# A fp32 decoder trunk on one core: eight pairs of weight tiles only in the FFNs, and four of eight k pairs in seven products in two of eleven groups

## The chip, the cores and the metric

The kernel runs on one core of one Trainium2 chip. The metric is the device time of one execution in microseconds (us); the time of a kernel is the median of its runs. A second number, the span, comes from one profiled execution and runs from its first to its last profiled instruction.

## What is computed

A decoder trunk over 256 positions of width 2048, all in float32: two layers, then a last RMSNorm.

```python
def swiglu(xn, w_gate, w_up, w_down):
    return (jax.nn.silu(xn @ w_gate) * (xn @ w_up)) @ w_down
...
for layer in range(DEPTH):                       # DEPTH = 2
    xn = rms_norm(h, norm_mix[layer])
    if layer % 2 == 0:
        mix = swa_mlstm_mixer(xn, w_in_even[j], w_out_even[j], ...)
    else:
        mix = forgetting_attention_mixer(xn, w_in_odd[j], fox_b_f[j], w_out_odd[j])
    h = h + mix
    h = h + swiglu(rms_norm(h, norm_ffn[layer]), w_gate[layer], w_up[layer], w_down[layer])
return rms_norm(h, norm_final)
```

The first mixer (the even layer) is sliding-window attention beside an mLSTM, the second (the odd layer) softmax attention with forget gates. Each ends in an output projection, `@ w_out`, 2048 to 2048. The FFN goes from 2048 to 5632 and back.

## The kernel before, in words

**Precision.** Every fp32 operand stands as two fp32r tiles, hi and lo. A weight chunk (256 rows by 512 columns, 512 KB) is loaded by SP into a raw tile (line 132; pool `wr`, four buffers). `split_chunk` (line 182) makes the pair: ACT copies raw to hi (line 185), DVE subtracts hi from raw to lo (line 186). A product of blocks is then three matmuls: hi·hi, hi·lo, lo·hi (lines 220 to 222 in `gemm`, lines 530 to 532 in `three`).

**Weight tiles.** `slot` (line 106) hands out the pairs of the list `weights` in turn. Six pairs are made once for the whole kernel, in pool `wp` (line 104). `close_layer` (line 762) opens the pool `fp0` or `fp1` of a layer's end, makes two more pairs there (hi6, lo6, hi7, lo7) and appends them to the list; then it runs `out_proj`, then `ffn`, then takes them off again. The pool of the layer's end opens while the mixer still works, in memory that it gives up; a tile whose memory is still read waits for the last reader.

**Output projection.** `out_proj` (line 508) works in 512-column blocks of w_out, two at a time: for both blocks the first 12 of the 16 k steps, then for both the last 4. A block is 8 chunks of 12 matmuls. Its left operand is mh and ml, the mixer's result, of which the early k steps (the attention heads) are there sooner than the late ones. Finished blocks are added to the residual (line 368), and xh and xl for the FFN are made of them by two batches of four transposing DMAs a block pair (`box`, line 315, on SP). The mixer's end in the even layer is the mLSTM (lines 1079 to 1130), whose output goes through transposing DMAs (`hv`, line 333) to mh (line 359); in the odd layer it is the softmax (lines 418 to 431), the transposes of its probabilities (lines 471 and 475) and the products with v (lines 485 and 486).

**FFN.** `ffn` (line 635) takes w_gate and w_up in 11 groups of 512 columns, in three parts (0 to 2, 3 to 6, 7 to 10); after each part come the down products of what is done. A group is a call of `pair_group` (line 537) over eight pairs of k steps. A plain pair is 24 matmuls. In a mixed pair the 2 x 2 blocks of the pair are multiplied in seven products in place of eight, 21 matmuls: DVE forms sums of the weight blocks (lines 605 to 608), of which one extra half tile and two full tiles are split (line 355) beside the usual split of one chunk. A mixed pair takes four pairs of weight tiles, a plain one two. The sums on the activation side (`sx`, `x4`) are made once a layer. At a group's end, `combine` (line 551) joins the seven-product banks and line 663 adds the plain banks. Plain and product banks are four PSUM banks each, which change roles from group to group (`bank`, line 534).

`ORDER` says which pairs are mixed and in what order they come; `HEAVY` has four mixed pairs, and a mixed pair first. `DENSE` names the groups that use HEAVY; it is empty, so that all use ORDER:

```python
ORDER = ((0, 0), (1, 1), (0, 2), (1, 3), (0, 4), (1, 5), (0, 6), (0, 7))
HEAVY = ((1, 1), (0, 0), (1, 3), (0, 2), (1, 5), (0, 4), (1, 7), (0, 6))
```

**Order of the work.** Each engine runs its instructions in program order, and that order is fixed when the program is built: the framework's scheduler interleaves them by when it takes tiles and operands to be free. So a change of which tile a chunk gets can reorder every engine.

Of the kernel before, what the change touches and what calls it, by code (L numbers as in the profile page):

```python
# [9 lines left out]
F32R = mybir.dt.float32r  # L10
# [7 lines left out]
P = 128  # L18
# [5 lines left out]
NB = 512  # L24
CK = 2
# [10 lines left out]
ORDER = ((0, 0), (1, 1), (0, 2), (1, 3), (0, 4), (1, 5), (0, 6), (0, 7))  # L36
HEAVY = ((1, 1), (0, 0), (1, 3), (0, 2), (1, 5), (0, 4), (1, 7), (0, 6))
FOURTH = 7
DENSE = ()
DOWN = {  # L40
    6: ((0, 0), (1, 1), (0, 2), (1, 3), (0, 4), (0, 5)),
    8: ((0, 0), (1, 1), (0, 2), (1, 3), (0, 4), (1, 5), (0, 6), (0, 7)),
# [26 lines left out]
def mixed_of(order):  # L69
    return [p for w, p in order if w]  # L70
# [5 lines left out]
def trunk(  # L76
# [23 lines left out]
    xl = sp_.tile([P, KT, S], F32R, name="xl")  # L100
    mh = sp_.tile([P, KT, S], F32R, name="mh")
    ml = sp_.tile([P, KT, S], F32R, name="ml")
    wp = ctx.enter_context(tc.tile_pool(name="wp", bufs=1))
    weights = [[wp.tile([P, CK, NB], F32R, name=f"{a}{i}") for a in ("hi", "lo")] for i in range(6)]

    def slot():
        weights.append(weights.pop(0))
        return weights[-1]

    wr = ctx.enter_context(tc.tile_pool(name="wr", bufs=4))  # L110
    cp = ctx.enter_context(tc.tile_pool(name="cp", bufs=1))
# [70 lines left out]
    def split_chunk(raw, n):  # L182
        hi, lo = slot()
        for k in (slice(0, 1), slice(1, CK)) if any(raw is f for f in fine) else (slice(0, CK),):
            latest[0] = nc.scalar.copy(hi[:, k, 0:n], raw[:, k, 0:n])  # L185
            nc.vector.tensor_tensor(  # L186
                out=lo[:, k, 0:n], in0=raw[:, k, 0:n], in1=hi[:, k, 0:n].bitcast(F32), op=ALU.subtract
            )
        return hi, lo
# [318 lines left out]
    def out_proj(w, idx, key, extra):  # L508
        last, rest = KT - 4, []
        for n0 in (0, 2):  # L510
            accs = [new_acc() for _ in range(2)]
            for i in range(2):
                gemm(accs[i], m_of, w, (n0 + i) * NB, NB, 0, last, KT, step=6 * i)
            for i in range(2):
                gemm(accs[i], m_of, w, (n0 + i) * NB, NB, last, KT, KT, step=6)
                add_out(accs[i], n0 + i)
                (later if n0 == 0 else rest).append(
                    (LATER[n0 + i], split_turned(idx, n0 + i, *scrap(extra[3], n0 + i), extra))
                )
                square_sum(key, n0 + i)  # L520
        return rest
# [15 lines left out]
    def pair_group(fp, par, lhs, sums, mats, order, todo=(), halves=None, inner=None, raws=None):  # L537
# [32 lines left out]
        for pos, (kind, pair) in enumerate(order):  # L570
# [21 lines left out]
            if first:  # L592
# [8 lines left out]
                else (t4[:, 0, :], t4[:, 1, :], ra[:, 0, :], ra[:, 1, :])  # L601
            )
            hu, lu = slot()
            split_plain(hu[:, 1, :], lu[:, 1, :], rb[:, 1, :])
            nc.vector.tensor_tensor(out=ta, in0=rb[:, 0, :], in1=ra[:, 0, :], op=ALU.subtract)
# [4 lines left out]
            for src in (ra, rb) if halves else (t4, ra):  # L610
                if halves:
                    hs, ls = halves.pop(0)
                    halves.append((hs, ls))
                else:
                    hs, ls = slot()
                split_plain(hs, ls, src)
                parts.append((hs, ls))
# [17 lines left out]
    def ffn(layer, fp, sx, x4, sd, key, todo, idx_next=None, key_next=None, finish=None):  # L635
# [8 lines left out]
        for g0, g1 in zip(PARTS, PARTS[1:]):  # L644
# [3 lines left out]
            for g in range(g0, g1):  # L648
# [6 lines left out]
                    [(w_gate[layer], g * NB), (w_up[layer], g * NB)],  # L655
                    HEAVY if g in DENSE else ORDER,
                    todo,
# [104 lines left out]
    def close_layer(layer, w_out, idx, key, **rest):  # L762
        with tc.tile_pool(name=f"fp{layer}", bufs=2) as fp:
            nx = len(mixed_of(ORDER))
            nd = max(len(mixed_of(o)) for o in DOWN.values())
            sx = [fp.tile([P, nx, 4, P], F32R, name=f"sx{i}", bufs=1) for i in range(2)]
            x4 = fp.tile([P, 2, P], F32R, name="x4", bufs=1)
            more = [[fp.tile([P, CK, NB], F32R, name=f"{a}{i}", bufs=1) for a in ("hi", "lo")] for i in (6, 7)]
            weights.extend(more)
            todo = out_proj(w_out, idx, key, (*sx, x4, fp))  # L770
            sd = [fp.tile([P, nd, 4, P], F32R, tag=f"sd{i}", name=f"sd{i}", bufs=1) for i in range(2)]
            ffn(layer, fp, sx, x4, sd, key, todo, **rest)
            for pair in more:
                weights.remove(pair)


    acc0 = new_acc()
    hi, lo = slot()
# [366 lines left out]
    for n in range(4):  # L1145
        nc.gpsimd.dma_start(h[:, :, n * NB : (n + 1) * NB], xv[:, :, n * NB : (n + 1) * NB])

    close_layer(0, w_out_even[0], 2, "f0", idx_next=1, key_next="m1")


# [140 lines left out]
    def finish(acc, n, gf):  # L1291
        for t in range(NT):
# [31 lines left out]
            nc.scalar.dma_start(ov[:, t, NB : 2 * NB], b1)  # L1324

    close_layer(1, w_out_odd[0], 3, "f1", finish=finish)


# [47 lines left out]
```

## Time and profile before

| | before |
|---|---|
| median of 3 runs | 2105.7 us (2105.07 to 2107.09) |
| the profiled execution | 2104.5 us, span 2102.8 us |
| mean granted TensorE clock | 0.993 |
| HBM read | 408.68 MB, 195 GB/s over the span |

How to read it: PE is TensorE's matmuls, PEld its weight loads (beside PE), DVE VectorE, ACT ScalarE, SP the engine that issues the DMAs; SPq marks an issue on it. A row of the timeline is start, duration, engine, line, operation, output tile <- input tiles; in brackets the idle time before it and what ended it. A row of a group of instructions is line, engine, operation, count | busy time, mean in ns | idle before, and what ended it. A row of waits is engine, tile and line that waited <- what it waited for: us in all, times, longest. A row of windows is the stretch and its length, then busy time (instructions) of PE, PEld, DVE, ACT and POOL, the granted clock, the share of the DMAs and GB/s. Of the 40 slices of the span, PE is at nine tenths or more in all but the fifth, the 26th and the last, and the granted clock in all but the 26th.

### The profile page before, as it was taken

What the parts mean: (1) busy time and instruction counts of PE and PEld (TensorE: products, weight loads), DVE (VectorE), ACT (ScalarE), POOL (GpSimd) and SP (SyncE); (2) the same over time, 40 slices, a digit from 0 to 9 for tenths busy, and PEclk for the clock granted to TensorE, in tenths of its full rate; (3) what the DMA queues carried; (4) which work ended last, traced back from release to release, by engine and by line L of the source; (5) the groups of instructions that cost most, each with busy time, mean ns of one, the idle gap of its engine ahead of it and who ended that gap; (6) DMA issues with size and microseconds to landing.
All of it is one profiled execution on the core that took longest, in us unless ns stands there. A gap on an engine that the chain in (4) does not pass through costs nothing.

```text
span 2102.8 us, 26924 instructions
## 1 busy us (share of the span) xinstructions
PE 2072.5 (99%) x9473; PEld 1718.5 (82%) x9473; DVE 1821.5 (87%) x2367; ACT 1373.8 (65%) x1744; POOL 41.4 (2%) x66
## 2 busy tenths in 40 slices
PE   9999899999999999999999999899999999999998
PEld 7878688888888888888888888688888888888887
DVE  6788668999999899999898778579999999899994
ACT  6767577665576656667676776577655667556763
POOL 1010100000000000000000000000000000000000
PEclk9999999999999999999999999899999999999999
DMA  8566577666677567766677866476756677666763
GB/s 291 178 200 200 170 230 218 214 210 200 207 224 227 185 202 227 229 202 181 213 214 193 242 184 193 135 237 204 240 192 225 196 209 225 216 200 206 224 193 139
DMA packets 309576, 434.87 MB, mean 207 GB/s; under 512 B 106413, under 2 KB 114625, under 8 KB 309313
## 3 DMA queue, kind: packets, MB, share of 16 engines
q1 hardware_dynamic: 307088, 426.27, 66.1%
q0 software_dynamic: 1632, 5.80, 0.8%
q8 instruction: 74, 1.21, 0.2%
q10 hardware_dynamic: 720, 1.09, 0.1%
q14 instruction: 62, 0.50, 0.1%
HBM read 408.68 MB, written 2.12 MB: 195 GB/s over the span
## 4 chain that ended last, share of the span: by engine, by line
PE 94%; ACT 2%; DVE 2%; DMA 1%; issue 1%; SPq 1%; POOLq 0%; POOL 0%; ACTq 0%; DVEq 0%
PE acc L530 20%; PE acc L531 20%; PE acc L532 20%; PE acc L221 5%; PE acc L220 5%; PE acc L222 5%; PE prod L530 5%; PE prod L532 5%; PE prod L531 5%; DVE lo L186 1%; PE p L384 1%; PE po L485 1%; ACT hi L185 1%; ACT s L418 0%; DMA raw<-in_w_out_odd_dram 0%
## 5 line engine op out<-in xcount | busy, mean ns | idle before, releaser
L186 DVE TENSOR_TENSOR lo<-raw,hi 128x1024 fp32r<-128x1024 f32 (+3 forms) x656 | 769.1, 1190 | 159.2 <-ACT hi L185 157.5
L185 ACT CAST hi<-raw 128x1024 fp32r<-128x1024 f32 (+3 forms) x656 | 662.4, 1027 | 353.9 <-PE acc L532 165.3
L531 PE MATMUL acc<-lo,xh 128*128 128x512 f32 x1320 | 513.9, 389 | 0.0
L532 PE MATMUL acc<-hi,xl 128*128 128x512 f32 x1320 | 511.2, 389 | 0.0
L530 PE MATMUL acc<-hi,xh 128*128 128x512 f32 x1320 | 506.2, 390 | 0.0
L532 PEld LDWEIGHTS acc<-hi,xl 128*128 128x128 f32 x1320 | 247.8, 188 | 51.4
L531 PEld LDWEIGHTS acc<-lo,xh 128*128 128x128 f32 x1320 | 247.8, 188 | 51.4 <-issue 0.2
L530 PEld LDWEIGHTS acc<-hi,xh 128*128 128x128 f32 x1320 | 247.8, 188 | 51.4 <-issue 0.2
L354 ACT CAST hi<-raw 128x512 fp32r<-128x512 f32 x204 | 166.9, 819 | 159.5 <-PE acc L532 80.7
L355 DVE TENSOR_TENSOR lo<-raw,hi 128x512 fp32r<-128x512 f32 x204 | 190.2, 932 | 14.0 <-ACT hi L354 12.8
L531 PE MATMUL acc<-lo,mh 128*128 128x512 f32 x466 | 181.3, 389 | 0.0
L532 PE MATMUL acc<-hi,ml 128*128 128x512 f32 x466 | 180.7, 389 | 0.0
L530 PE MATMUL acc<-hi,mh 128*128 128x512 f32 x466 | 176.8, 390 | 1.3 <-ACT hi L185 1.3
L354 ACT CAST hi<-t 128x1024 fp32r<-128x1024 f32 x95 | 100.0, 1053 | 68.6 <-PE acc L532 40.7
L220 PE MATMUL acc<-hi,mh 128*128 128x512 f32 (+1 forms) x322 | 125.4, 393 | 7.8 <-ACT mh L359 7.3
L355 DVE TENSOR_TENSOR lo<-t,hi 128x1024 fp32r<-128x1024 f32 x95 | 115.7, 1218 | 16.1 <-ACT hi L354 15.8
L221 PE MATMUL acc<-lo,mh 128*128 128x512 f32 (+1 forms) x322 | 126.0, 392 | 0.1
L222 PE MATMUL acc<-hi,ml 128*128 128x512 f32 (+1 forms) x322 | 124.5, 392 | 0.0
L530 PEld LDWEIGHTS acc<-hi,mh 128*128 128x128 f32 x466 | 87.3, 188 | 20.2 <-ACT hi L185 2.2
L532 PEld LDWEIGHTS acc<-hi,ml 128*128 128x128 f32 x466 | 87.5, 188 | 18.2
L531 PEld LDWEIGHTS acc<-lo,mh 128*128 128x128 f32 x466 | 87.5, 188 | 18.2
L221 PE MATMUL acc<-lo,xh 128*128 128x512 f32 (+3 forms) x288 | 99.7, 347 | 0.2 <-DVE lo L186 0.2
(356 smaller groups left out, 3171.2 us busy)
## 6 DMA issues: line engine op xcount, KB each, us to landing
raw<-in_w_gate_dram SPq DMA_DIRECT2D x176, 512.0 KB, 4.4
raw<-in_w_up_dram SPq DMA_DIRECT2D x176, 512.0 KB, 4.7
raw<-in_w_down_dram SPq DMA_DIRECT2D x176, 512.0 KB, 4.7
raw<-in_w_in_odd_dram SPq DMA_DIRECT2D x88, 512.0 KB, 5.1
raw<-in_w_in_even_dram SPq DMA_DIRECT2D x51, 512.0 KB, 4.8
raw<-in_w_out_even_dram SPq DMA_DIRECT2D x32, 512.0 KB, 4.5
raw<-in_w_out_odd_dram SPq DMA_DIRECT2D x32, 512.0 KB, 4.4
hr<-in_w_in_even_dram SPq DMA_DIRECT2D x12, 512.0 KB, 4.5
```

Of the source, the lines that this page charges most:

```text
L185: latest[0] = nc.scalar.copy(hi[:, k, 0:n], raw[:, k, 0:n])
L186: nc.vector.tensor_tensor(out=lo[:, k, 0:n], in0=raw[:, k, 0:n], in1=hi[:, k, 0:n].bitcast(F32), op=ALU.subtract)
L220: nc.tensor.matmul(o, ah[:, ts], hi, start=(k == 0), stop=False)
L221: nc.tensor.matmul(o, ah[:, ts], lo, start=False, stop=False)
L222: nc.tensor.matmul(o, al[:, ts], hi, start=False, stop=(k == k_all - 1 and cs.stop == n))
L354: nc.scalar.copy(dst_h, src)
L355: nc.vector.tensor_tensor(out=dst_l, in0=src, in1=dst_h.bitcast(F32), op=ALU.subtract)
L384: nc.tensor.matmul(pq[j % 2][:, j // 2, :], q_of(j, b), k_of(j)[:, 0:cols], start=True, stop=True)
L485: nc.tensor.matmul(po, v_of(j, 0), tt[:, j, 0:2, :].rearrange("p c q -> p (c q)"), start=True, stop=False)
L530: nc.tensor.matmul(o, ah, hi, start=start, stop=False)
L531: nc.tensor.matmul(o, ah, lo, start=False, stop=False)
L532: nc.tensor.matmul(o, al, hi, start=False, stop=stop)
```

## The change

Two things. `slot` draws from a list `stock` when there is one, and else allocates a pair from `wp`, which now has six buffers of two tags. The list is filled only for the FFN: the two more pairs are made after `out_proj`, not ahead of it, put into it with the six, and it is cleared after `ffn`. And `DENSE` names groups 4 and 8.

```diff
-DENSE = ()
+DENSE = (4, 8)
...
-    wp = ctx.enter_context(tc.tile_pool(name="wp", bufs=1))
-    weights = [[wp.tile([P, CK, NB], F32R, name=f"{a}{i}") for a in ("hi", "lo")] for i in range(6)]
+    wp = ctx.enter_context(tc.tile_pool(name="wp", bufs=6))
+    stock = []
 
     def slot():
-        weights.append(weights.pop(0))
-        return weights[-1]
+        if not stock:
+            return [wp.tile([P, CK, NB], F32R, tag=a, name=a) for a in ("hi", "lo")]
+        stock.append(stock.pop(0))
+        return stock[-1]
...
-            more = [[fp.tile([P, CK, NB], F32R, name=f"{a}{i}", bufs=1) for a in ("hi", "lo")] for i in (6, 7)]
-            weights.extend(more)
             todo = out_proj(w_out, idx, key, (*sx, x4, fp))
             sd = [fp.tile([P, nd, 4, P], F32R, tag=f"sd{i}", name=f"sd{i}", bufs=1) for i in range(2)]
+            more = [[fp.tile([P, CK, NB], F32R, name=f"{a}{i}", bufs=1) for a in ("hi", "lo")] for i in range(2)]
+            stock.extend(more + [slot() for _ in range(6)])
             ffn(layer, fp, sx, x4, sd, key, todo, **rest)
-            for pair in more:
-                weights.remove(pair)
+            stock.clear()
```

## The prediction

> **What bounds the kernel now.** I read the page first: busy times, the chain that ended last, the costliest groups.
>
> ```profile
> span 2102.8 us, 26924 instructions
> PE 2072.5 (99%) x9473; PEld 1718.5 (82%) x9473; DVE 1821.5 (87%) x2367; ACT 1373.8 (65%) x1744; POOL 41.4 (2%) x66
> ...
> PE 94%; ACT 2%; DVE 2%; DMA 1%; issue 1%; SPq 1%; POOLq 0%; POOL 0%; ACTq 0%; DVEq 0%
> ...
> L185 ACT CAST hi<-raw 128x1024 fp32r<-128x1024 f32 (+3 forms) x656 | 662.4, 1027 | 353.9 <-PE acc L532 165.3
> ```
>
> PE is busy for 99% of the span and makes 94% of the chain. ACT, which feeds the weight tiles, has 165.3 us of its idle time ended by a matmul that gave a tile back: the split is ahead of PE, and the number of tiles is what holds it. So there are two ways to less time: fewer matmuls, and the places where PE stands or runs slowly. The view of waits, for PE, names these:
>
> ```profile
> PE pp L471 <- DVE s L431: 9.5, 1, 9.5
> PE acc L220 <- ACT mh L359: 7.3, 1, 7.3
> PE acc L530 <- ACT hi L185: 1.3, 2, 0.7
> ```
>
> Two stalls make up 16.8 us; nothing else is above 1.3 us. Both lie in out_proj, where the end of the mixer and the output projection overlap. Four windows, for the even and the odd layer: first out_proj's first two blocks with the mixer's end, then its other two.
>
> ```profile
> 227.20:291.20 64.00, 55.01 (x234) 43.79 (x233) 37.21 (x71) 34.07 (x65) 2.80 (x4) 0.92 0.52 168
> 291.20:334.70 43.50, 43.50 (x194) 36.03 (x193) 30.75 (x44) 32.83 (x47) 0.00 (x0) 1.00 0.83 254
> 1294.40:1362.20 67.80, 58.27 (x268) 48.60 (x269) 37.93 (x57) 38.95 (x61) 0.63 (x1) 0.90 0.48 144
> 1362.20:1405.70 43.50, 43.50 (x193) 36.04 (x192) 29.68 (x38) 28.18 (x37) 0.00 (x0) 1.00 0.80 263
> ```
>
> The second block of two takes 43.5 us at a granted clock of 1.00. The same work beside the mixer takes 64.0 and 67.8 us, at 0.92 and 0.90, and neither DVE, ACT nor the DMAs (0.52, 0.48) are full. The mixer's own matmuls are in these windows too (42 and 76 of the 234 and 268, as 192 belong to the two blocks).
>
> **Part one: the stock only in the FFNs.** Before, the seventh and eighth pair (hi6/lo6, hi7/lo7) join the ring ahead of out_proj. Their memory lies where the mixer's last tiles still are: by the addresses of the built program, og, dt_ and hr in the even layer, qtf, ktf, vtail and tt in the odd one. The ring is strictly in order, six pairs, then these two. The first four chunks of weight block 0 (k 0 to 7) and then the first chunks of block 1 come up, and the two pairs fall to block 1, k 0 to 3. Their casts must wait for the mixer's end. Rows of SP and PE in the even layer, then of PE and ACT in the odd one:
>
> ```profile
> 227.42 15.35 SPq L132 DMA_DIRECT2D raw<-in_w_out_even_dram  x5
> 245.84 10.34 SPq L333 DMA_TRANSPOSE hv<-room  x8
> 256.23 33.17 SPq L132 DMA_DIRECT2D raw<-in_w_out_even_dram  x12
> ```
>
> ```profile
> 254.85 0.79 PE L220 MATMUL acc<-hi,mh 128*128 128x512 f32 x1 [7.30 <-ACT mh L359]
> 255.44 0.63 PE L221 MATMUL acc<-lo,mh 128*128 128x512 f32 x1
> ...
> 258.43 0.57 PE L220 MATMUL acc<-hi,mh 128*128 128x512 f32 x1
> 258.84 0.39 PE L221 MATMUL acc<-lo,mh 128*128 128x512 f32 x1
> ```
>
> ```profile
> 1317.72 0.40 PE L222 MATMUL acc<-hi,ml 128*128 128x512 f32 x1
> 1327.64 1.45 PE L471 MATMUL pp<-ident,s 128*128 128x128 f32 x4 [9.53 <-DVE s L431]
> ...
> 1334.67 0.38 PE L486 MATMUL po<-tt,vtail 128*128 128x128 f32 x2
> ```
>
> ```profile
> 1335.57 2.01 ACT L185 CAST hi<-raw 128x1024 fp32r<-128x1024 f32 x2
> ```
>
> In the odd layer the two casts run back to back at 1335.57, 0.9 us after the last reader of vtail: they had been waiting for that memory, with the raw tiles landed, and two of the four raw buffers were stuck behind them. PE meanwhile had only block 0 to do, and ran out of it.
>
> After, out_proj has six pairs, none of them in the mixer's memory. In the order of PE's instructions of the changed program, 48 matmuls of block 1 (k 0 to 7) now stand ahead of the instruction that stalled in the even layer, and 58 stand ahead of or between the pp transposes of the odd layer. Before, none did. The price of a matmul is the pitch of an FFN group, where PE never waits:
>
> ```profile
> 592.50:634.00 41.50, 41.50 (x185) 34.38 (x184) 39.85 (x50) 28.40 (x32) 0.00 (x0) 1.00 0.71 214
> ...
> 716.50:757.90 41.40, 41.40 (x184) 34.28 (x183) 37.58 (x43) 21.36 (x24) 0.00 (x0) 1.00 0.62 195
> ```
>
> A group is 5 x 24 + 3 x 21 = 183 matmuls in 41.5 us, or 0.2268 us each. So 48 fill 10.9 us and 58 fill 13.2 us, each more than its stall (7.3, 9.5). Even layer (where the wait is for mh, behind the eight transposes of hv on SP): 7.3 us of idle go, and with them the slow stretch behind them, where matmuls start 0.43 us apart (255.44 to 258.43: seven or eight in 3.0 us) instead of 0.2268: another 1.4 us. Gain 8.7 us. Odd layer: 9.5 us go. The transposes and po matmuls behind it (1327.64 to 1334.85, 7.2 us) run, I estimate, at the same half pace, so that 3.6 us of them are slowness; the 58 matmuls reach past the stall by 13.2 − 9.5 = 3.7 us, and I take 2.6 of the 3.6. Gain 12.1. The sum is **−20.8 us**. The bounds: nothing, if the chain of the mixer's end is made longer by as much (below); and, if every idle and slow microsecond of the two windows went, even 64.00 − 55.01 + 1.4 = 10.4 and odd 67.80 − 58.27 + 3.6 = 13.1, −23.5 in all.
>
> The new splits sit among the mixer's last operations on ACT and DVE: four chunks more, at 1.03 (ACT) and 1.22 us (DVE). Both engines idle for longer than that in the stalls (37.21 and 34.07 busy of 64), so they find room; what they push back is covered by 10.9 − 7.3 = 3.6 us, and 3.7 us in the odd layer. This is why I cost it at nothing.
>
> What out_proj loses is two of eight pairs in its second half. In SP's order the eight box transposes now come together, where there were four, a load, and four:
>
> ```profile
> 289.72 5.13 SPq L315 DMA_TRANSPOSE box<-box  x4
> 294.96 0.51 SPq L132 DMA_DIRECT2D raw<-in_w_out_even_dram  x1
> 295.58 5.12 SPq L315 DMA_TRANSPOSE box<-box  x4
> ```
>
> ```profile
> raw<-in_w_out_even_dram SPq DMA_DIRECT2D x32, 512.0 KB, 4.5
> ```
>
> For 10.3 us no load leaves SP. PE eats a chunk (12 matmuls) in 2.72 us, so 3.8 chunks go. The load behind the block needs 4.5 us to land, 1.03 for the cast and 1.22 for the subtract, 6.8 us, and by the order it leaves about 7 us ahead of its matmul. The cost is 0 to 4 us in a layer; I take 1.2, as the lead just covers it: **+2.4 us**.
>
> **Part two: groups 4 and 8 with four mixed pairs.** A mixed pair has seven block products, 21 matmuls, a plain one 24. Two groups in each of two layers: 12 matmuls fewer, **−2.7 us**. The fourth pair's activation sums (FOURTH) are worked out before too. What it adds is on DVE:
>
> ```profile
> L355 DVE TENSOR_TENSOR lo<-t,hi 128x1024 fp32r<-128x1024 f32 x95 | 115.7, 1218 | 16.1 <-ACT hi L354 15.8
> ...
> L355 DVE TENSOR_TENSOR lo<-raw,hi 128x512 fp32r<-128x512 f32 x109 | 74.6, 685 | 12.6 <-ACT hi L354 12.0
> L608 DVE TENSOR_TENSOR raw<-raw 128x512 f32<-128x512 f32 x109 | 74.5, 683 | 0.6
> ...
> L607 DVE TENSOR_TENSOR raw<-raw,t 128x512 f32<-128x512 f32 x95 | 64.9, 683 | 0.6
> ...
> L663 DVE TENSOR_TENSOR c<-acc,c 128x512 f32<-128x512 f32 x88 | 58.0, 679 | 0.0
> ```
>
> ```profile
> 618.72 1.22 DVE L355 TENSOR_TENSOR lo<-raw,hi 128x1024 fp32r<-128x1024 f32 x1
> 619.85 2.35 DVE L186 TENSOR_TENSOR lo<-raw,hi 128x1024 fp32r<-128x1024 f32 x2
> ```
>
> ```profile
> 625.76 0.39 PE L531 MATMUL prod<-lo,sx 128*128 128x512 f32 x1
> ```
>
> A mixed pair is three subtractions of 1.22, one of 0.69 and four of 0.68 us (7.1 us); a plain pair is two of 1.22. One after the other they start about 0.08 us before the last has ended (618.72 to 619.85 is 1.13), so the difference is about 4.2 us. A group's DVE work goes from 39.85 to 44.0 us, while PE's goes from 41.5 to 40.8: DVE falls back by 3.2 us in each of these groups. Its smallest lead in an ordinary group is the one shown: the split that ends at 619.94 is first read at 625.76, 5.8 us. So 2.6 us are left, and the next groups give back 41.5 − 39.85 = 1.65 each, the down products 41.4 − 37.58 = 3.8. There are two ordinary groups and the down products before group 8, two behind it. I cost DVE at nothing; if the cover is gone, it is up to 4.2 us in each of four groups, 16.6 us. ACT, at 28.40 of 41.50, has room for the added casts.
>
> **Sum.** −20.8 + 2.4 − 2.7 = −21.1. The profiled execution took 2104.5 us (span 2102.8 and 1.7 around it): 2083.4. It was 1.2 us below the median of 2105.7, so against that I forecast **2084.6 us**.
>
> **The rivals.** What a measurement of this kernel can tell from no change is 0.2%, 4.2 us; so faster means below 2101.5, slower above 2109.9.
>
> *DVE sets the pace in the four dense groups* (0.14): the full 16.6 us land on PE, 2084.6 + 16.6 = 2101.2, on the edge of faster. For it: DVE is at 39.85 of 41.50 already, and a group that begins with a mixed pair needs the last group's banks at once. Against it: a lead of 5.8 us, and 3.2 to be lost.
>
> *Six pairs starve out_proj* (0.09). Two pairs less are 2 x 2.72 = 5.4 us of cover. If PE waits for that much in both layers at the box transposes, and as much once more where the FFN starts, the time grows by 4 x 5.4 − 2.4 = 19.2 to 2103.8, no difference; with half as much it is 2094.2. "Perfetto Trace Analysis" of the Trainium skill (section Optimization Strategy) says that a gap which keeps coming back can mean that there is no room for the next tile, so buffer count is what to raise; by that alone, a lower count here would bring gaps. The trace does not show this for out_proj: its two gaps stand where two tiles of eight could not be used.
>
> *The stalls stay* (0.06): the chain through mh and s is moved back by the splits as far as PE got ahead, and only the matmuls saved are left: 2105.7 − 2.7 = 2103.0, the same.
>
> *The drain loop, slower* (0.08). At a dense group's start, DVE must add the last group's four banks (L663, 4 x 0.68) after PE has ended it, then split the first mixed pair (7.1 less the overlaps, 6.5) before PE can go on: 9.2 us with PE idle, at start and end of four dense groups. It decides from the point where DVE's lead at a boundary is under 3.2 us. With six such waits of eight (55.2 us less the 21.1, so 2139.8) the kernel is slower; with three it is 2112.2, with two, 2103.0. The order on PE, where plain matmuls of the new group stand ahead of its first mixed ones, speaks against it.
>
> **How the numbers follow.** The forecast keeps 0.63. Faster: 0.63, 0.09 of the first rival's 0.14 (any partial price), 0.06 of the second's 0.09: 0.78. Same: 0.06 + 0.05 + 0.03 = 0.14. Slower: 0.08. The forecast alone reaches from 2079.5 (all 23.5 us and the 2.7 gained, nothing lost at the boxes) to about 2092 (8 us more lost at boxes and DVE). The range goes from 2076, some 3 us below the lowest, for clock losses in the windows that I did not see, to 2101, which takes in the partial prices; it leaves out the slower case and the unchanged ones.
>
> **What would show it.** In the waits of PE, the rows pp L471 and acc L220 fall from 9.5 and 7.3 to under 2; the windows of out_proj's first half shorten from 64.0 and 67.8 to about 55 each at a clock near 1.00; PE has 12 instructions fewer; a dense group takes 40.8 us with no wait on lo. I am wrong if PE waits for lo or hi in groups 4 and 8 (DVE), if waits on hi with raw from w_out stand behind the box transposes (slots), or if the stalls only move to another mh.

## The result and the profile after

The changed kernel takes 2078.5 us (median; 2078.0 to 2078.6) against 2105.4 for the kernel before: a ratio of 0.987 (0.9853 to 0.9887), 26.9 us less. The forecast was 2084.6, 21.1 us less than the 2105.7 shown then. The span goes from 2102.8 to 2076.7 us, by 26.1.

The page of the changed kernel, its span, busy times and the chain that ended last:

```profile
span 2076.7 us, 26845 instructions
## 1 busy us (share of the span) xinstructions
PE 2064.6 (99%) x9461; PEld 1712.5 (82%) x9461; DVE 1833.4 (88%) x2391; ACT 1379.3 (66%) x1752; POOL 45.8 (2%) x66
...
PE 89%; DVE 4%; DMA 3%; ACT 2%; issue 2%; SPq 0%; POOLq 0%; POOL 0%; ACTq 0%; DVEq 0%
```

The idle time of PE (span less busy) goes from 30.3 to 12.1 us, and its busy time falls by 7.9, although only 12 matmuls of 0.2268 us (2.7 us) are gone. The other 5.2 are time in which matmuls ran slowly or one by one; most of it stood behind the two stalls, where the clock was low (3.2 and 1.9 us, worked out further down). The waits of PE in the changed kernel, its largest rows (tile, line, what it waited for: us, times, longest):

```profile
PE cold L170 <- POOL ones L167: 1.2, 1, 1.2
PE prod L532 <- DVE xl L362: 1.0, 1, 1.0
PE acc L532 <- ACT hi L187: 1.0, 3, 0.4
```

Both stalls, 9.5 and 7.3 us, are gone; a wait on xl is new. The windows of the changed kernel, for the same stretches as before: out_proj of the even layer, its first and second half; the end of layer 0's FFN with the start of layer 1; the odd mixer; out_proj of the odd layer, both halves. (Lines of the changed kernel are one or two higher than before.)

```profile
227.20:279.20 52.00, 52.00 (x236) 43.08 (x235) 35.14 (x70) 30.80 (x60) 2.80 (x4) 1.00 0.56 193
279.20:322.70 43.50, 43.50 (x194) 36.02 (x193) 31.40 (x45) 34.70 (x49) 0.00 (x0) 1.00 0.82 264
924.50:1010.80 86.30, 84.74 (x376) 69.14 (x376) 80.43 (x100) 57.07 (x75) 0.00 (x0) 1.00 0.57 179
1010.80:1282.90 272.10, 271.78 (x1327) 229.72 (x1326) 228.14 (x310) 194.54 (x265) 18.69 (x13) 1.00 0.71 210
1282.90:1337.80 54.90, 54.90 (x271) 46.37 (x270) 35.32 (x50) 30.61 (x48) 1.05 (x1) 1.00 0.55 175
1337.80:1381.30 43.50, 43.50 (x193) 36.05 (x192) 33.05 (x47) 35.87 (x52) 0.00 (x0) 1.00 0.84 268
```

The two of these that were not shown of before:

```profile
938.50:1022.30 83.80, 83.80 (x375) 69.42 (x375) 77.44 (x97) 56.02 (x75) 0.00 (x0) 1.00 0.58 175
1022.30:1294.40 272.10, 271.70 (x1328) 229.71 (x1326) 228.83 (x311) 192.85 (x264) 14.40 (x13) 1.00 0.73 211
```

And the dense group 4 with the ordinary group 5 behind it, in the changed kernel:

```profile
552.50:593.30 40.80, 40.80 (x181) 33.79 (x181) 38.55 (x50) 28.60 (x32) 0.00 (x0) 1.00 0.66 213
593.30:634.80 41.50, 41.50 (x184) 34.38 (x184) 40.26 (x52) 29.67 (x32) 0.00 (x0) 1.00 0.69 221
```

Set against each other, stage by stage:

| stage | before | after | difference |
|---|---|---|---|
| out_proj even, first half | 64.0 | 52.0 | −12.0 |
| out_proj even, second half | 43.5 | 43.5 | 0 |
| out_proj odd, first half | 67.8 | 54.9 | −12.9 |
| out_proj odd, second half | 43.5 | 43.5 | 0 |
| four dense groups | 41.5 each | 40.8 each | −2.7 |
| end of layer 0, start of layer 1 (the seam) | 83.8 | 86.3 | +2.5 |
| odd mixer | 272.1 | 272.1 | 0 |
| the down products before group 3, and group 3, both layers | | | −1.0 |

The last row compares the ends of the last matmuls of groups 2 and 3: 105.9 and 106.0 us before, 105.2 and 105.7 after. Two waits on hi, 0.6 and 0.7 us, stood there; one of 0.4 us is left. The rows sum to −26.1, which is the whole difference of the spans.

### The profile page after: what moved, and what is told of

Its sections match the earlier page's. It is cut to its first block, busy times and chain, and to the rows that moved or that the text cites. A ratio compares the mean times of both kernels' runs of the same rounds, so it can differ in the third digit from the quotient of the medians.

```text
span 2076.7 us, 26845 instructions
## 1 busy us (share of the span) xinstructions
PE 2064.6 (99%) x9461; PEld 1712.5 (82%) x9461; DVE 1833.4 (88%) x2391; ACT 1379.3 (66%) x1752; POOL 45.8 (2%) x66
## 4 chain that ended last, share of the span: by engine, by line
PE 89%; DVE 4%; DMA 3%; ACT 2%; issue 2%; SPq 0%; POOLq 0%; POOL 0%; ACTq 0%; DVEq 0%
PE acc L532 19%; PE acc L533 19%; PE acc L534 19%; PE acc L223 5%; PE acc L222 5%; PE acc L224 5%; PE prod L532 5%; PE prod L533 5%; PE prod L534 5%; DVE lo L188 1%; DMA raw<-in_w_in_odd_dram 1%; ACT hi L187 1%; DMA raw<-in_w_down_dram 1%; PE p L386 1%; PE po L487 0%
## 5 line engine op out<-in xcount | busy, mean ns | idle before, releaser
L533 PE MATMUL acc<-lo,xh 128*128 128x512 f32 x1296 | 504.6, 389 | 0.0
L534 PE MATMUL acc<-hi,xl 128*128 128x512 f32 x1296 | 501.7, 389 | 0.0
L532 PE MATMUL acc<-hi,xh 128*128 128x512 f32 x1296 | 487.4, 390 | 0.0
L534 PEld LDWEIGHTS acc<-hi,xl 128*128 128x128 f32 x1296 | 243.3, 188 | 50.5
L533 PEld LDWEIGHTS acc<-lo,xh 128*128 128x128 f32 x1296 | 243.3, 188 | 50.4 <-issue 0.2
L356 ACT CAST hi<-raw 128x512 fp32r<-128x512 f32 x212 | 172.8, 819 | 83.0 <-PE acc L534 60.0
L357 DVE TENSOR_TENSOR lo<-raw,hi 128x512 fp32r<-128x512 f32 x212 | 198.8, 940 | 6.3 <-ACT hi L356 6.3
L532 PE MATMUL acc<-hi,mh 128*128 128x512 f32 x466 | 171.0, 390 | 1.0 <-ACT hi L187 1.0
L357 DVE TENSOR_TENSOR lo<-t,hi 128x1024 fp32r<-128x1024 f32 x99 | 121.2, 1224 | 10.5 <-ACT hi L356 10.2
L223 PE MATMUL acc<-lo,mh 128*128 128x512 f32 (+1 forms) x322 | 126.3, 392 | 0.0
```

The source lines that it names most:

```text
L223: nc.tensor.matmul(o, ah[:, ts], lo, start=False, stop=False)
L356: nc.scalar.copy(dst_h, src)
L357: nc.vector.tensor_tensor(out=dst_l, in0=src, in1=dst_h.bitcast(F32), op=ALU.subtract)
L532: nc.tensor.matmul(o, ah, hi, start=start, stop=False)
L533: nc.tensor.matmul(o, ah, lo, start=False, stop=False)
L534: nc.tensor.matmul(o, al, hi, start=False, stop=stop)
```

## The experiments

**Theory A**, that of the prediction: the two more pairs stood in memory that the mixer still used, and as the ring is in order, they held up the output projection behind them. **Rivals**: the gain needs both edits together (B); it comes from pool tiles in place of a fixed list, which let the scheduler order the work otherwise (C); fewer pairs are better in themselves, or their number does not matter (D). The kernel before was run anew beside each set of experiments, with a median of 2104.2 to 2105.4 us in the five sets, so medians of kernels of different sets compare to about 1 us; the spans and stages are compared beside them.

**The stock alone.** `DENSE = ()` in the changed kernel.

```diff
-DENSE = (4, 8)
+DENSE = ()
```

> The stock alone, no dense group (all groups in ORDER). Theory A (the two pairs in the mixer's memory held up out_proj): the windows of out_proj's first halves stay at 52.0 and 54.9 us and the whole time is that of the changed kernel plus the 12 matmuls, 2078.5 + 2.7 = 2081.2 us; if the 2.5 us lost between the layers in the changed kernel come from its dense group 8, they come back too, 2078.7. Theory B (the two edits need each other, the dense groups using room that the stock gives): 2090 or more.

Measured: 2077.5 us (2076.6 to 2078.4), 0.9874 (0.9859 to 0.9889) of before; span 2076.7, the same as with both edits. The whole gain is the stock's; B falls. The seam costs nothing here (84.0 us from the first matmul of its down products to the first of layer 1, as before, and 86.5 in the changed kernel), so it is the dense groups that lose 2.5 us there, about as much as they save.

**The dense groups alone**, on the kernel before.

```diff
-DENSE = ()
+DENSE = (4, 8)
```

> The four dense groups alone, on the kernel before with its ring of eight. Theory A: the two stalls of 9.5 and 7.3 us stay, 12 matmuls go, 2105.4 - 2.7 = 2102.7 us. Rival (DVE sets the pace in dense groups): up to 4.2 us of waits on lo or hi in each of four groups, 2107 to 2119 us.

Measured: 2104.9 us, a ratio of 1.000 (0.9991 to 1.0009): no gain at all, on either kernel. The profile has the old stalls, and at the seam it has what the changed kernel has; windows of the even out_proj's first half and of the seam:

```profile
227.20:291.90 64.70, 55.58 (x240) 44.41 (x240) 37.94 (x71) 34.71 (x66) 2.81 (x4) 0.95 0.52 171
...
937.40:1022.90 85.50, 84.39 (x376) 69.20 (x375) 79.80 (x99) 56.97 (x74) 0.00 (x0) 1.00 0.58 176
```

The groups save their 2.7 us, the seam takes 1.7 back (83.8 to 85.5), and the two first halves come out 0.7 and 0 us longer.

**The list joined late.** The kernel before, with the two pairs made after `out_proj`.

```diff
-            more = [[fp.tile(...) for a in ("hi", "lo")] for i in (6, 7)]
-            weights.extend(more)
             todo = out_proj(w_out, idx, key, (*sx, x4, fp))
             sd = [...]
+            more = [[fp.tile(...) for a in ("hi", "lo")] for i in (6, 7)]
+            weights.extend(more)
             ffn(layer, fp, sx, x4, sd, key, todo, **rest)
```

> The kernel before with one edit: the two more pairs are made after out_proj and join the same list there; six pairs from fixed tiles in out_proj, no pool tiles, no dense group. Theory A (what counts is that no pair of out_proj stands in the mixer's memory): as the stock alone, about 2081 us, no wait of 7 or 9 us. Rival C (what counts is that the tiles come from a pool, so that the scheduler orders them otherwise): as before, 2105 us.

Measured: 2081.3 us, 0.9893 (0.9876 to 0.9909), no wait above 1.2 us. C falls as the main cause: fixed tiles and the old list give 23 of the 27 us. The first halves, even and odd:

```profile
227.20:280.40 53.20, 52.22 (x233) 42.57 (x231) 34.86 (x69) 32.19 (x63) 3.78 (x4) 1.00 0.59 193
...
1283.20:1338.10 54.90, 54.86 (x268) 46.34 (x269) 34.41 (x48) 31.21 (x48) 0.63 (x1) 1.00 0.56 175
```

The even one takes 53.2 where the pool has 52.0: PE waits once for a lo (0.6) and once for a hi (0.4) there. Another 0.9 us stand in the first part of the odd layer's FFN, 125.2 us from the last matmul of `out_proj` to the first of the down products, where the stock alone has 124.3. Together that is the 2.1 us by which the spans differ (2078.8 and 2076.7). Why the pool avoids these is not shown.

**The two pairs two places sooner** in the ring of before.

```diff
-            weights.extend(more)
+            weights[2:2] = more
```

> The kernel before with one edit: the two more pairs join the ring two places ahead of its six last turns are over, at the third and fourth place in place of the seventh and eighth. Theory A: they fall to block 0, k 4 to 7, so PE runs out of matmuls four chunks (block 0, k 4 to 11 of the odd layer) or two chunks (even layer) sooner: 24 to 48 matmuls, 5.4 to 10.9 us a layer, more idle at the mixer's end, about 2115 to 2125 us. Rival C (the place does not matter): 2105 us.

Measured: 2113.1 us (2110.8 to 2113.6), 1.0041 (1.0026 to 1.0056): slower, by 8.5 us. The direction is A's, the size is below its range (2115 to 2125), as only the even layer pays. The first halves, even and odd:

```profile
227.20:300.60 73.40, 57.45 (x234) 45.44 (x233) 40.17 (x74) 35.66 (x65) 2.80 (x4) 0.88 0.47 153
...
1303.20:1371.00 67.80, 60.15 (x272) 48.69 (x271) 38.52 (x51) 34.04 (x50) 0.63 (x1) 0.95 0.47 152
```

64.0 goes to 73.4, while the odd half keeps its 67.8 us with the idle time in other places. I had counted the chunks that are held up, not what other chunks PE could take in their place. In the odd layer the wait on s shrinks from 9.5 to 4.1 us while waits on hi come up elsewhere, so PE had other chunks there.

**Four pairs in out_proj**, on the list joined late.

```diff
+            kept = [weights.pop() for _ in range(2)]
             todo = out_proj(w_out, idx, key, (*sx, x4, fp))
+            weights.extend(kept)
```

> The kernel with the list joined late (six pairs in out_proj), with two of the six set aside during out_proj, so that four are left. Theory A: in a strict ring of n pairs, the chunks of block 0 that wait for the mixer's end hold their pairs; with six, block 1 gets four chunks done (48 matmuls, 10.9 us) ahead of it, with four, two chunks (24 matmuls, 5.4 us, less than the stalls of 7.3 and 9.5 us). So 2 to 6 us a layer come back as waits in the first halves, and the loads in the second half, which I had feared for six pairs, now starve: 2086 to 2100 us against 2081. Rival D (fewer pairs in out_proj are better in themselves, or their number does not matter): 2081 or less.

Measured: 2095.3 us, 0.9959 (0.9944 to 0.9974), 14 us over six pairs; D falls. The windows of out_proj, four of them:

```profile
227.20:284.90 57.70, 53.99 (x234) 43.90 (x233) 33.56 (x68) 31.67 (x63) 2.80 (x4) 0.97 0.51 162
284.90:328.60 43.70, 43.70 (x194) 36.20 (x193) 29.01 (x40) 32.07 (x44) 0.00 (x0) 1.00 0.81 249
1293.30:1348.20 54.90, 54.87 (x268) 46.31 (x269) 32.29 (x46) 29.61 (x46) 0.63 (x1) 1.00 0.51 156
1348.20:1392.60 44.40, 43.66 (x191) 35.51 (x191) 29.68 (x41) 32.73 (x47) 0.00 (x0) 1.00 0.83 260
```

Even with four pairs the first halves (57.7, 54.9) are far shorter than with eight of which two stood in the mixer's memory (64.0, 67.8). The even one loses 4.5 us against the list joined late (53.2), within the 2 to 6 that I had reckoned for a layer. The odd one loses nothing (54.9 in both), where I had reckoned that 24 matmuls could not cover 9.5 us: how many chunks of block 1 fit ahead of the mixer's end is not what decides there. The second halves, which I had expected to starve, lose 0 and 0.7 us. From the last matmul of `out_proj` to the first of the down products, 127.8 and 128.7 us stand against 124.5 and 125.2, so 3.3 and 3.5 us go where the FFN starts; that I had not reckoned with. Together this makes 12 of the 14.8 us between the spans (2093.6 and 2078.8); the rest was not followed up.

**Eight pairs in the second half only.** The two pairs join the list when blocks 2 and 3 begin.

```diff
         for n0 in (0, 2):
+            if n0 == 2:
+                weights.extend(joined)
```

> The kernel before with one edit: the two more pairs, made ahead of out_proj as before, join the list at the start of its second half (blocks 2 and 3), when the mixer is done. Six pairs beside the mixer, eight behind the box transposes. If six pairs are enough there, as the second half's 43.5 us in the changed kernel says: as the list joined late, 2081 us. If the 2.4 us that I charged for six pairs behind the box transposes are real: about 2079.

Measured: 2081.3 us, 0.9889 (0.9873 to 0.9906), span 2078.8, both the same as with six pairs throughout. The 2.4 us that I charged for six pairs behind the box transposes do not exist.

**Which dense group costs the seam.** The changed kernel with one dense group a layer: 4, 8 or 7.

```diff
-DENSE = (4, 8)
+DENSE = (4,)
```

> The changed kernel with group 4 alone in HEAVY: 6 matmuls fewer than with the stock alone. If the 2.5 us lost between the layers come from DVE's debt of group 8 (two groups and a down product ahead of that place), they are gone: 0.68 us a group, 2077.45 - 1.4 = about 2076.1 us, a span near 2075.3. If any dense group upsets the order there: about 2078.5.

> The changed kernel with group 8 alone in HEAVY. If DVE's debt of group 8 is the cause of the loss between the layers: 2077.45 - 1.4 + 2.5 = about 2078.6 us, with the wait of prod on xl in the profile. If group 4 is needed for it: 2076.1.

> The changed kernel with group 7 alone in HEAVY, in place of group 8. Debt of DVE (3.2 us fall back, 1.65 us a group come back): one ordinary group more ahead of the seam, so the loss there shrinks from 2.7 to about 1.0 us, 2077.45 - 1.4 + 1.0 = 2077.0. Order rival (any dense group in the last part upsets the order that the scheduler writes for the seam): the loss stays at 2 us or more, 2078.6.

Measured: group 4, 2076.8 us (2076.2 to 2077.4), span 2074.8; group 8, 2078.6 (2078.2 to 2079.1), span 2077.1; group 7, 2077.8 (2077.1 to 2078.9), span 2076.0. By the spans, of one execution each, group 4 gains 1.9 us over the stock alone (2076.7), group 7 0.7, and group 8 loses 0.4; by the medians (2077.5 there), group 4 gains 0.7, and groups 7 and 8 lose 0.4 and 1.2. The runs of one of these kernels differ by 0.9 to 1.8 us among themselves, so the totals alone do not settle it. The stage says more: from the end of group 10 of layer 0 to the end of the first half of the odd out_proj there are 411.3 us in the stock alone, 410.8 with group 4, 411.5 with group 7, 413.0 with group 8, and 413.3 in the changed kernel with 4 and 8. Group 8 costs 1.75 us there, group 7 0.3. One ordinary group more ahead of the seam takes the loss down by 1.5 us, near the 1.65 that I gave a group. That speaks for DVE's debt, and against the rival that any dense group in the last part upsets the order there. A wait that stands at the seam in the kernel with group 8 alone:

```profile
PE prod L532 <- DVE xl L362: 1.7, 1, 1.7
```

In the changed kernel it stands as 1.0 us. With group 7 alone it stands too, as 1.1 us, at a loss of only 0.3, so its length is not the loss. At the seam, PE needs the next layer's xl, which DVE can only make after the last residual sums. DVE's rows there, in the changed kernel, then in the stock alone:

```profile
972.74 2.49 DVE L370 TENSOR_TENSOR h<-acc,h 128x512 f32<-128x512 f32 x4
...
983.04 0.87 DVE L362 SCALAR_TENSOR_TENSOR xl<-pt,gT,xh 128x256 fp32r<-128x256 f32 x2
```

```profile
971.12 1.28 DVE L370 TENSOR_TENSOR h<-acc,h 128x512 f32<-128x512 f32 x2
...
977.65 0.87 DVE L362 SCALAR_TENSOR_TENSOR xl<-pt,gT,xh 128x256 fp32r<-128x256 f32 x2
```

The residual sums end at 975.2 in place of 972.4, and the first xl comes 5.4 us later, although group 10 had ended 1.15 us sooner (924.48 and 925.63). Ten microseconds of this stretch, at the same distance from the end of group 10, in the changed kernel and in the stock alone:

```profile
975.00:985.00 10.00, 10.00 (x50) 8.16 (x48) 8.28 (x12) 10.00 (x17) 0.00 (x0) 1.00 0.26 55
```

```profile
976.10:986.10 10.00, 10.00 (x46) 8.28 (x45) 9.63 (x16) 9.51 (x14) 0.00 (x0) 1.00 0.41 125
```

In the changed kernel ACT is busy for all of it, and DVE idles for 1.7 us, waiting for ACT's hi. DVE's instructions also stand in another order: the residual sums come four in a row, where the stock alone has two and two. So the loss sits at the seam and goes with the dense group close ahead of it; how much of it is DVE's debt, how much ACT and how much the order, these runs do not show.

**Four dense groups in a row.** `DENSE = (3, 4, 5, 6)`.

> The changed kernel with four dense groups in a row (3 to 6) in each layer. By the sum of the prediction DVE falls back 3.2 us a group and 12.8 in all, of which its lead of 5.8 covers less than half: about 7 us of waits of PE on lo or hi in each layer against 2.7 us gained, 2077.45 + 2 x 4.3 = about 2086 us. If DVE is never the limit (rival): 2077.45 - 5.4 = 2072.

Measured: 2096.3 us, 0.996 (0.9945 to 0.9975), 18.8 over the stock alone where I had reckoned 8.6. Groups 4, 5 and 6 of layer 0:

```profile
552.20:595.50 43.30, 42.27 (x186) 34.51 (x185) 40.56 (x52) 28.59 (x33) 0.00 (x0) 1.00 0.60 185
595.50:639.00 43.50, 42.43 (x178) 32.47 (x177) 43.50 (x57) 31.19 (x35) 0.00 (x0) 1.00 0.69 206
639.00:684.20 45.20, 42.44 (x181) 33.20 (x180) 44.10 (x56) 29.56 (x34) 0.00 (x0) 1.00 0.67 207
```

An ordinary group has 41.5 us, a dense one alone 40.8. Group 3, the first of the row, is still free: with the down products ahead of it, it takes 1.1 us less than in the stock alone (104.75 and 105.83 us). The second, third and fourth are not. By the fourth, PE goes at DVE's pace, 45.2 us a group with DVE busy for 44.1 of them: near the 44.0 us of DVE work that the prediction gave a dense group. This is the rival in which DVE sets the pace. PE's waits in this kernel are on ACT's hi (4.5 us) as well as on DVE's lo (1.9), but ACT is busy for only 29.56 of the 45.20 us. The lead carries one dense group, not two.

**Placed by layer.** HEAVY in groups 1 and 4 of layer 0 and 1, 4 and 8 of layer 1; then in group 4 of layer 0 and 4 and 8 of layer 1, `DENSE = ((4,), (4, 8))`. The edit of the first:

```diff
-DENSE = (4, 8)
+DENSE = ((1, 4), (1, 4, 8))
...
-                    HEAVY if g in DENSE else ORDER,
+                    HEAVY if g in DENSE[layer] else ORDER,
```

> The changed kernel with HEAVY in groups 1 and 4 of layer 0 and 1, 4 and 8 of layer 1 (no dense group in the last part ahead of the seam between the layers). If a dense group is worth its three matmuls (0.68 us) wherever an ordinary group and the down products follow and nothing new starts behind them: group 4 alone gave 2076.8; three groups more, 3 x 0.68 = 2.0: 2074.7 us, a span near 2072.8. If group 1 of a part of three groups costs the next down products as much as group 8 costs the seam: 2077 to 2080.

> The changed kernel with group 8 in HEAVY in layer 1 only, and group 4 in both layers. In layer 1 nothing new starts behind the FFN, so group 8 keeps its 0.68 us; in layer 0 the loss at the seam goes. Sum: group 4 alone gave a span of 2074.8 us and 2076.8; 0.7 less, a span near 2074.1 and a time near 2076.1 us. If the loss at the seam is not group 8's: a span of 2076 or more.

Measured: with group 1, 2083.0 us (2081.1 to 2085.8; span 2079.3), a miss: a dense group 1 takes 41.9 us in layer 0, with PE idle for 1.3 of them. From the last matmul of `out_proj` to the first of the down products there are 126.0 and 126.3 us, in layer 0 and 1, where the second kernel has 124.3 in both. That DVE has as yet no lead there, so soon behind the start of the FFN, would explain it, but was not followed up.

```profile
365.10:407.00 41.90, 40.60 (x178) 33.00 (x177) 41.61 (x53) 29.46 (x32) 0.00 (x0) 1.00 0.70 209
```

Without it, 2076.0 us (2075.7 to 2077.0), span 2074.2, 0.9867 (0.985 to 0.9883) of before: as forecast, and the lowest of all kernels here, 2.5 us below the changed kernel both in span and in median. Group 4 alone, at 2076.8 us, is within the scatter of it.

## Why the prediction was right, and where it was not

**The main step held.** The stock alone gives the gain; moving the two blocked pairs sooner makes the kernel slower; the old list without them in out_proj is fast. This carries more than the rows of the two casts in the prediction: they start at 1335.57, 0.5 us after the end of vtail's last reader (1334.67 and 0.38), right behind ACT's cast before them, so the trace names no wait of theirs. The new splits did not push the mixer's end back: from the start of its window, the odd layer's probabilities are reached after 31.4 us (1314.30 − 1282.90) against 32.8 (1327.21 − 1294.40). The rows, before and after:

```profile
1327.21 1.92 DVE L431 TENSOR_SCALAR s<-s,rec 128x128 f32<-128x128 f32 x8
```

```profile
1314.30 1.93 DVE L433 TENSOR_SCALAR s<-s,rec 128x128 f32<-128x128 f32 x8
```

**Even layer, −8.7 forecast, −12.0 measured: the term that was too small**, and past the bound of 10.4. I took the one stall of 7.3 us and three microseconds of slow matmuls behind it. The kernel before, cut finer:

```profile
237.20:247.40 10.20, 8.69 (x37) 6.33 (x35) 7.00 (x23) 4.75 (x15) 1.42 (x2) 1.00 0.50 161
247.40:254.90 7.50, 0.20 (x2) 0.05 (x1) 1.83 (x8) 3.25 (x8) 0.00 (x0) 0.58 0.21 45
254.90:260.00 5.10, 5.10 (x17) 4.07 (x18) 3.29 (x9) 3.79 (x11) 0.69 (x1) 0.62 0.48 128
```

All 9.0 us of idle go, 1.5 of them small waits in front of the stall (10.20 − 8.69), where block 1's matmuls now stand between the mixer's. The slow stretch costs 5.1 x 0.38 = 1.9 us, not 1.4. That is 10.9. Some of the other 1.1 us stand in front of the stall, where the mixer's pairs of matmuls come one by one:

```profile
240.31 0.60 PE L1091 MATMUL pom<-ce,qst 128*128 128x257 f32 x2
240.75 0.59 PE L1081 MATMUL pc<-ve,kw 128*128 128x257 f32 x2
...
242.11 0.60 PE L1089 MATMUL pom<-ve,dt__1179 128*128 128x257 f32 x2
243.38 0.67 PE L1089 MATMUL pom<-ve,dt__1179 128*128 128x257 f32 x2 [0.68 <-DVE hv L1097]
243.89 0.60 PE L1091 MATMUL pom<-ce,qst 128*128 128x257 f32 x2
244.32 0.60 PE L1081 MATMUL pc<-ve,kw 128*128 128x257 f32 x2
244.95 0.67 PE L1089 MATMUL pom<-ve,dt__1179 128*128 128x257 f32 x2
246.42 0.70 PE L1089 MATMUL pom<-ve,dt__1179 128*128 128x257 f32 x2 [0.80 <-DVE st L1093]
```

Where work follows at once, a pair takes 0.44 us (240.31 to 240.75). The six pairs from 242.11 on hold PE for 3.35 us up to 246.96, where six times 0.44 would be 2.6: 0.7 us. The last 0.4 are not accounted for.

**Odd layer, −12.1 forecast, −12.9 measured.** The stretch behind the stall, 1327.6 to 1335, had a mean granted clock of 0.57, near the half pace that I had estimated:

```profile
1327.60:1335.00 7.40, 7.36 (x29) 6.22 (x30) 2.39 (x9) 1.76 (x3) 0.00 (x0) 0.57 0.00 0
```

7.4 x 0.43 = 3.2 us of slowness and 9.5 of idle make 12.7. The clock was 0.50 up to 1334.0, for 6.4 us, and 1.00 from there; behind the even stall it was 0.50 for 4.0 us, from 254.85 to 258.81. "TensorE: Matmul & The Clock Gate" of the Trainium skill (Part 1, the HAM clock gate) has the array at half rate after an idle window of about 3.4 us and at full rate after a busy window of the same length, and says that the window runs free, whatever the kernel does. The trace agrees with the length and the free run (last section), but the clock fell already 1.0 and 2.2 us after PE's last matmul, and there the measurement decides.

**Boxes, +2.4 forecast, 0 measured.** Both second halves stay at 43.5 us, and two pairs more change nothing. The working itself had the load leave 7 us ahead of a matmul that needs 6.8, so the 1.2 us a layer were caution and not a cost that its rows gave.

**Matmuls, −2.7 forecast, −2.7 measured**: a dense group takes 40.8 us, without a wait.

**DVE at nothing: the step that failed**, in its place more than in its size. DVE's busy time grows by 13.6 us over the stock alone (1819.8 to 1833.4), 3.4 a dense group, where the working had 4.2. Its count of the groups is off by one, as three ordinary groups (5, 6 and 7) and the down products lie ahead of group 8; two lie behind it. The debt of group 8 was to be worked off by these two and the down products behind them. It was not: 2.5 us were lost at the seam, nearly as much as the matmuls gained, and group 7 in its place loses 0.3. I asked whether DVE's lead lasts through the dense group and not what must be done next that cannot be done ahead. That the loss goes with group 8 is shown; that it is DVE's debt alone is not.

The errors, −3.3 (even), −0.8 (odd), −2.4 (boxes), +2.5 (seam) and −1.0 (two waits on hi that I had left out), sum to −5.0: −21.1 becomes −26.1. So the total was near partly because errors of both signs stood in it. The two first halves gained 24.9 us, more than the bound of 23.5, and the range holds the result because it reached 3 us further for clock losses that I had not seen; 0.5 us of such losses came, in the even layer, and 0.7 us of matmuls that came one by one. The drain loop, the stalls that stay and six starving pairs did not appear.

## What to carry to other kernels

A ring of buffers that is served in order is as good as its worst buffer: two more, in memory that the stage before still reads, cost 23 us, and six free ones were enough. When buffers come and go with a stage, look at who last reads the memory that they are given, not only at their number. When an edit loads an engine that has a lead, follow the debt to the next work that cannot be done ahead; here the loss turned up there, two groups after the edit.

## What the runs showed of the hardware that was not expected

In these traces the granted clock had two values, 1.00 and 0.50, at the stalls, and the times between its changes were whole multiples of 3.41 us. In the kernel before, in windows of 0.1 us, it fell at 248.57 and rose at 258.81 around the even stall, and fell at 1320.36 and rose at 1334.01 around the odd one: 10.24 and 13.65 us, three and four times 3.41. With the dense groups alone, the same two stalls have 6.83 and 10.24 us, two and three times 3.41. Behind the stalls the half pace lasted 4.0 and 6.4 us in the one kernel and 3.4 and 4.5 in the other, for the same instructions. So it is not the kind of work alone that sets it, but also where a stall falls between these fixed points. The kernel before in such stretches, behind the odd stall:

```profile
1327.19:1330.60 3.41, 2.96 (x13) 2.56 (x14) 1.92 (x8) 0.59 (x1) 0.00 (x0) 0.50 0.00 0
1330.60:1334.01 3.41, 3.41 (x12) 2.72 (x12) 0.69 (x1) 0.59 (x1) 0.00 (x0) 0.50 0.00 0
1334.01:1337.43 3.42, 3.42 (x18) 2.94 (x18) 2.16 (x3) 2.92 (x4) 0.00 (x0) 1.00 0.00 0
```

Behind a stretch with PE busy for 2.96 us the clock stayed low, and behind one with 3.41 it rose. It had fallen behind stretches in which PE was still busy for 1.16 us (odd) and 1.60 us (even) of 3.41. A stall of 9.5 us so cost 12.7.
